# The w_down sums of a Strassen-like feed-forward: half of them beside attention, the rest in smaller steps, and a layer norm on three engines

## The chip, the cores and the metric

The kernel runs on one core of a Trainium2 chip. Its engines have instruction streams of their own: TensorE (PE in the profile, its weight loads PEld), VectorE (DVE), ScalarE (ACT), GpSimd (POOL) and SyncE (SP), which here issues all DMA transfers, in its own order. The metric is the device time in microseconds (us); lower is better. The comparison is by the median of several runs.

## The reference, cut to what matters

One layer of a decoder with 2048 tokens of width 1024, all in float32: four mixers, of which three feed `ymix` and the dilated attention feeds the rest of the columns, then an output projection, a layer norm, a feed-forward of width 4096 with a squared ReLU, and a second layer norm.

```python
mix = jnp.concatenate([y_a, y_b, y_c, y_d], axis=-1).astype(x.dtype) @ w_out[l]
x = _layer_norm(ALPHA * x + mix, ln1_w[l], ln1_b[l])
h = jnp.square(jax.nn.relu(x @ w_up[l]))
x = _layer_norm(ALPHA * x + h @ w_down[l], ln2_w[l], ln2_b[l])
```

## The kernel before, in words

Every matrix product runs as three products of rounded parts: an operand is split by ACT into a high part (names ending in `h`) and by VectorE or POOL into the rest (ending in `l`); the helper `split` (L169) gives every third rest to POOL. Elementwise helpers record all their operations in one line each: L115 for additions, subtractions and products of two tiles, L128 for the form with a scalar (`stt`), L131 and L135 for ACT, L112 for matrix products.

The order of the instructions is set by a scheduler that reads the program as it is written and places each instruction by its own estimate of when operands and buffers are free; what is written earlier has the higher priority. So a step written late may stand early on a queue, and the other way round. Engines then run their streams in that order. DMA is issued by SP alone.

The stages after the mixers:

- Attention (up to about 1690 us in the profile). `weave` puts steps of other work between its units: `out_part(t)` multiplies the first three mixers' columns of token tile t by `w_out` (six of the eight row blocks), and `out_final(t)` adds attention's columns, forms the first layer norm and stores the tile and its transpose (`x1`, `x1T`). A unit loads its values as `av`.
- The up projection, `ffn_up`, twice, for one half of the tokens each (1767 to 2493 us). It is a two-by-two scheme with seven products P1 to P7 in place of eight; the sums of operands are formed by VectorE and POOL. Each half has 16 steps `s`, one for 128 columns and their partner. A step loads four pieces of `w_up` (`wr`), forms sums, splits seven weights, runs seven products of 12 matrix instructions each, and stores seven results to DRAM (`H7`, in the trace `H0P..` and `H1P..`). A step starts its chain with a copy of P1 out of PSUM to `q`. The functions `mid(s)` and `between(s)` are called inside and behind a step, and run a step of another generator there.
- `ffn_x1`: sums and splits of the second half's inputs, behind the steps 8 to 11 of the first half.
- `ffn_t`: for each of 16 rows f it loads four pieces of `w_down` (`b12`, `t1`, `b22`, `b21`), forms four differences, and stores them as P5, P7, P6 and P4 in `TD` (the trace says `TDP`). It has two steps a row (load, then form and store). Three of its four buffers are `xr`, of which there are three; the fourth is `x1t`.
- The down projection, `ffn_down` (2493 us to the end): 32 steps of seven products each, 16 for each half of the tokens. Inputs are read back from `H7` and split (`hh`, `hl`), the weights of a product (`x0h`, `x1h` and so on) are exchanged every fourth step, each product at an offset of its own (`OFF`). The sums of products are added to `y`, which starts as ALPHA times the residual `x1`: ACT scales it on arrival, POOL adds `t`, `u2` or `u3` (the tiles `wh`), VectorE adds a product out of PSUM. Four groups of tokens go through four steps each in a half; in the last of them `lnorm2` runs on two tiles of 128 tokens, and the result is stored. Its `y` is then loaded with the residual of the other half.

Of the kernel before, what the change touches and what calls it, by code (L numbers as in the profile page):

```python
# [18 lines left out]
P = 128  # L19
# [65 lines left out]
class Body:  # L85
# [1006 lines left out]
    def out_open(self, es, ef):  # L1092
# [3 lines left out]
        self.zF = [self.dp.tile([P, D], F32, name=f"zF{t}") for t in range(seq // P)]  # L1096
        self.xT = [self.dp.tile([KT, P, 512], F32, name=f"x1T{i}") for i in range(seq // 512)]
# [76 lines left out]
    def ffn_open(self, es):  # L1174
# [8 lines left out]
        self.TD = {n: [self.dp.tile([P, 512], F32, name=f"TD{n}_{f}") for f in range(16)] for n in ("P4", "P5", "P6", "P7")}  # L1183
# [163 lines left out]
    def ffn_t(self):  # L1347

        nc, w = self.nc, self.ap["w_down"]
        for f in (12, 13, 14, 15, *range(12)):  # L1350
            b12, t1, b22 = self.raw(w[f][:, 512:]), self.raw(w[f][:, :512]), self.raw(w[f + 16][:, 512:])
            b21 = self.t(self.of, "x1t", [P, 2, 512], bufs=1)[:, 0]
            nc.sync.dma_start(b21, w[f + 16][:, :512])
            yield
            self.sub("v", t1, b12, t1)
            nc.sync.dma_start(self.TD["P5"][f], t1)
            self.sub("g", b12, b22, b12)
            nc.sync.dma_start(self.TD["P7"][f], b12)
            self.sub("v", b22, b22, t1)
            nc.sync.dma_start(self.TD["P6"][f], b22)  # L1360
            self.sub("g", b21, b21, b22)
# [6 lines left out]
    OFF = {"P1": 1, "P6": 1, "P2": 2, "P4": 2, "P5": 3, "P3": 3, "P7": 0}  # L1368

    def ffn_down(self):  # L1370

        nc, tc, of = self.nc, self.tc, self.of
        nsteps = 32
        wtag = lambda n: "x1" if n in ("P1", "P6", "P4", "P3") else "x0"
        chunk = lambda n, i: (i - self.OFF[n]) // 4 % 4
        with ExitStack() as es:
# [66 lines left out]
            for n, place in zip(("P1", "P6", "P2", "P5", "P7", "P4", "P3"), places):  # L1443
                if place == "xr":
                    W[n] = [self.split_to(wtag(n), r) for r in load_w(n, chunk(n, 0), place)]
                else:
                    split_w(n, list(load_w(n, chunk(n, 0), place)))
                if n == "P2":
                    for m in range(7):
                        load_h(m)  # L1450
                    lns = self.t(of, "ln1", [P, 2, D], bufs=1)
                    nc.sync.dma_start(lns, self.ap["lns"][2:4].partition_broadcast(P))
                    split_h(0)
                    split_h(1)
                elif n == "P7":
                    split_h(2)
                    split_h(3)
# [5 lines left out]
            for i in range(nsteps):  # L1463
# [50 lines left out]
def body(ctx, tc, ap, seq=SEQ):  # L1514
# [34 lines left out]
    def run(it):  # L1549
        for _ in it:  # L1550
            pass
# [138 lines left out]
```

## Time and profile before

| | |
|---|---|
| time, three runs | 3149.95 us median (3141.89 to 3160.94) |
| the profiled execution | 3160.75 us; its span, first to last instruction, 3159.0 us |
| PE | 2910.0 us busy, 92% of the span |
| VectorE, ACT, POOL | 69%, 43% and 50% |
| mean granted clock of TensorE | 0.927 |
| DMA | 513.71 MB, 163 GB/s in the mean |

Times within a stage are counted from the start of the span. Lines of the profile name an engine, a line of the source, the tile written and the tiles read, the count and a duration; a time in brackets is how long the engine stood idle before, and behind the arrow what ended it. Tables by stretch give the busy time of each engine, the granted clock as a share of full speed, and the mean busy share of the 16 DMA engines.

### The profile page before, as it was taken

The page shows a single profiled execution, that of the slowest core. Times are in us where ns is not written, and L with a number is a line of the kernel's source. Part 1 is how long each engine was busy: PE and PEld are TensorE (multiplying, and loading weights), DVE is VectorE, ACT ScalarE, POOL GpSimd, SP SyncE. Part 2 cuts the span into 40 slices and gives each one's busy share as a digit, 9 for nine tenths or more (in the row PEclk, how much of TensorE's full clock was granted, in tenths as well). Part 3 has the DMA queues.
Part 4 walks back from the last instruction along what each step waited for, and adds up shares of the span by engine and source line. Part 5 has one row for each costly group of instructions (what it writes and reads, how often), then busy time and mean ns, then how long its engine had stood idle before and what let it go on. Part 6 is the DMA issues. An engine that isn't in the chain of part 4 may idle for free. (4 is left out here: it accounts for less than half of the span.)

```text
span 3159.0 us, 46740 instructions
## 1 busy us (share of the span) xinstructions
PE 2910.0 (92%) x15524; PEld 2362.1 (75%) x15524; DVE 2193.9 (69%) x3828; ACT 1353.0 (43%) x2910; POOL 1571.1 (50%) x1432
## 2 busy tenths in 40 slices
PE   8889989889899999899998699898999899999997
PEld 6567777777778778777777578676778688877885
DVE  3457589776977865533445767778777677798878
ACT  3335333433443353334334354444354554454444
POOL 1333366454735645300123745556655476667765
PEclk9899798987999999699998799999999899999998
DMA  5344323333333354443455556777875766676653
GB/s 174 125 119 109 104 88 100 116 99 79 112 106 106 108 157 136 149 132 123 148 174 166 183 175 201 246 225 236 283 220 158 264 225 190 191 230 217 213 189 128
DMA packets 406657, 513.71 MB, mean 163 GB/s; under 512 B 34320, under 2 KB 234128, under 8 KB 406160
## 3 DMA queue, kind: packets, MB, share of 16 engines
q1 hardware_dynamic: 406416, 510.72, 52.0%
q8 instruction: 123, 2.02, 0.3%
q14 instruction: 118, 0.97, 0.1%
HBM read 354.69 MB, written 155.91 MB: 162 GB/s over the span
## 5 line engine op out<-in xcount | busy, mean ns | idle before, releaser
L112 PE MATMUL mm<-xh,wh 128*128 128x512 f32 x672 | 282.8, 423 | 33.3 <-ACT xh L135 17.8
L112 PE MATMUL mm<-xl,wh 128*128 128x512 f32 x672 | 282.1, 420 | 5.6 <-DVE xl L115 3.0
L112 PE MATMUL mm<-xh,wl 128*128 128x512 f32 x672 | 278.7, 415 | 2.7 <-DVE wl L115 2.6
L112 PE MATMUL bank<-x1h,hh 128*128 128x512 f32 x512 | 201.4, 393 | 16.9 <-ACT hh L135 12.3
L135 ACT ACTIVATE wh<-raw 128x512 fp32r<-128x512 f32 (+1 forms) x220 | 136.5, 629 | 172.2 <-DMA raw<-in_w_ch 68.8
L115 POOL TENSOR_TENSOR y<-y,wh 128x512 f32<-128x512 f32 x112 | 175.0, 1573 | 63.5 <-DVE wh L115 36.3
L112 PE MATMUL bank<-x1h,hl 128*128 128x512 f32 x512 | 200.9, 392 | 4.5 <-DVE hl L115 2.7
L112 PE MATMUL bank<-x1l,hh 128*128 128x512 f32 x512 | 200.9, 392 | 0.0
L112 PE MATMUL bank<-x0h,wh 128*128 128x512 f32 x384 | 159.2, 415 | 39.1 <-DVE c L115 30.5
L112 PEld LDWEIGHTS mm<-xh,wh 128*128 128x128 f32 x672 | 133.1, 198 | 73.5 <-ACT xh L135 22.8
L115 DVE TENSOR_TENSOR wl<-raw,wh 128x512 fp32r<-128x512 f32 (+1 forms) x146 | 124.4, 857 | 71.0 <-ACT wh L135 68.5
L115 POOL TENSOR_TENSOR wl<-raw,wh 128x512 fp32r<-128x512 f32 (+1 forms) x74 | 104.6, 1415 | 131.0 <-ACT wh L135 118.4
L112 PE MATMUL mm<-wh,xh 128*128 128x256 f32 (+1 forms) x512 | 156.9, 309 | 7.4 <-ACT stg L131 4.1
L112 PEld LDWEIGHTS mm<-xl,wh 128*128 128x128 f32 x672 | 132.9, 198 | 39.6 <-DVE xl L115 6.0
L112 PE MATMUL mm<-wl,xh 128*128 128x256 f32 (+1 forms) x512 | 156.7, 307 | 4.3 <-DVE wl L115 3.4
L112 PEld LDWEIGHTS mm<-xh,wl 128*128 128x128 f32 x672 | 132.7, 197 | 34.5 <-DVE wl L115 3.9
L112 PE MATMUL bank<-x0l,wh 128*128 128x512 f32 x384 | 156.4, 408 | 0.0
L112 PE MATMUL bank<-x0h,wl 128*128 128x512 f32 x384 | 155.8, 406 | 0.0
L112 PE MATMUL mm<-wh,xl 128*128 128x256 f32 (+1 forms) x512 | 154.4, 303 | 0.0
L112 PE MATMUL bank<-x0h,hh 128*128 128x512 f32 x384 | 150.4, 392 | 2.2 <-DVE y L128 1.3
L112 PE MATMUL bank<-x1h,wh 128*128 128x512 f32 x384 | 150.3, 392 | 2.1 <-ACT q L135 2.1
L112 PE MATMUL bank<-x0h,hl 128*128 128x512 f32 x384 | 150.3, 392 | 1.8 <-DVE hl L115 1.8
(466 smaller groups left out, 8801.9 us busy)
## 6 DMA issues: line engine op xcount, KB each, us to landing
raw<-in_w_ch SPq DMA_DIRECT2D x140, 256.0 KB, 3.0
wr<-in_w_up SPq DMA_DIRECT2D x128, 256.0 KB, 3.3
wl<-TDP SPq DMA_DIRECT2D x128, 256.0 KB, 3.5
wl<-in_w_down SPq DMA_DIRECT2D x104, 256.0 KB, 3.5
chF<-stg SPq DMA_DIRECT2D x68, 256.0 KB, 2.4
xraw<-in_xT SPq DMA_DIRECT2D x64, 256.0 KB, 3.7
z<-H0P SPq DMA_DIRECT2D x64, 256.0 KB, 4.1
z<-H1P SPq DMA_DIRECT2D x64, 256.0 KB, 3.8
```

What stands on the lines that cost most here:

```text
L112: return self.nc.tensor.matmul(out, lhsT, rhs, start=start, stop=stop)
L115: (self.nc.gpsimd if eng == "g" else self.nc.vector).tensor_tensor(out, a, b, op=op)
L135: self.nc.scalar.activation(out, in_, AF.Copy)
```

## The change

- `ffn_t` takes a list of rows and a mode. Rows 12 to 15 and 0 to 3 are formed in attention's first `weave`, by four steps in each of eight `out_part`s, in the two `z2` tiles, with all four subtractions on POOL. Rows 4 to 11 stay in the up projection with VectorE and POOL as before. A row now has four steps in place of two: load two pieces; subtract, store P5 and load the other two; subtract twice and store P7 and P6; subtract and store P4.
- In the up projection 12 of the remaining 32 steps are called in the first half and 20 in the second half's steps 2 to 11, two a step. Before these were 12 and 20 of 32 steps that were twice as long.
- At the start of `ffn_down` the inputs are loaded behind the second weight, and one input is split behind each of the second to fifth weights. P7 is prepared before P5; their `OFF` values are exchanged.
- The layer norm's weights (`lns`) are loaded in step 2, as written.
- The residual is no longer scaled by ACT. In the first step of a group the accumulation itself multiplies by ALPHA, and POOL's add follows it; in later steps the add comes first.
- `lnorm2` centres with ACT, scales with VectorE (`stt`, by the deviation and the weight), and adds the bias on VectorE for the first half of the columns and on POOL for the second.

```diff
-    def ffn_t(self):
+    def ffn_t(self, fs, up):
         nc, w = self.nc, self.ap["w_down"]
-        for f in (12, 13, 14, 15, *range(12)):
-            b12, t1, b22 = self.raw(w[f][:, 512:]), self.raw(w[f][:, :512]), self.raw(w[f + 16][:, 512:])
-            b21 = self.t(self.of, "x1t", [P, 2, 512], bufs=1)[:, 0]
+        e = "v" if up else "g"
+        for f in fs:
+            if up:
+                b12, t1, b22 = (self.t(self.fr, "xr", [P, 512], bufs=3) for _ in range(3))
+                b21 = self.t(self.of, "x1t", [P, 2, 512], bufs=1)[:, 0]
+            else:
+                (b12, t1), (b22, b21) = ((z[:, 0], z[:, 1]) for z in (self.t(self.of, "z2", [P, 2, 512], bufs=2) for _ in range(2)))
+            nc.sync.dma_start(b12, w[f][:, 512:])
+            nc.sync.dma_start(t1, w[f][:, :512])
+            yield
+            self.sub(e, t1, b12, t1)
+            nc.sync.dma_start(self.TD["P5"][f], t1)
+            nc.sync.dma_start(b22, w[f + 16][:, 512:])
             nc.sync.dma_start(b21, w[f + 16][:, :512])
             yield
-            self.sub("v", t1, b12, t1)
-            nc.sync.dma_start(self.TD["P5"][f], t1)
             self.sub("g", b12, b22, b12)
             nc.sync.dma_start(self.TD["P7"][f], b12)
-            self.sub("v", b22, b22, t1)
+            self.sub(e, b22, b22, t1)
             nc.sync.dma_start(self.TD["P6"][f], b22)
+            yield
             self.sub("g", b21, b21, b22)
             nc.sync.dma_start(self.TD["P4"][f], b21)
             yield
...
-    OFF = {"P1": 1, "P6": 1, "P2": 2, "P4": 2, "P5": 3, "P3": 3, "P7": 0}
+    OFF = {"P1": 1, "P6": 1, "P2": 2, "P4": 2, "P7": 3, "P3": 3, "P5": 0}
...
-            for n, place in zip(("P1", "P6", "P2", "P5", "P7", "P4", "P3"), places):
+            for q, (n, place) in enumerate(zip(("P1", "P6", "P2", "P7", "P5", "P4", "P3"), places)):
+                rs = load_w(n, chunk(n, 0), place)
...
-                if n == "P2":
+                if q == 1:
                     for m in range(7):
                         load_h(m)
-                    lns = self.t(of, "ln1", [P, 2, D], bufs=1)
-                    nc.sync.dma_start(lns, self.ap["lns"][2:4].partition_broadcast(P))
-                    split_h(0)
-                    split_h(1)
-                elif n == "P7":
-                    split_h(2)
-                    split_h(3)
+                if 0 < q < 5:
+                    split_h(q - 1)
...
-                            self.act(y[l][j], y[l][j], AF.Copy, scale=ALPHA)
-
-                def acc(l, j, ps, last=True):
-                    self.stt(y[l][j], y[l][j], 1.0, ps, ALU.mult, ALU.add, stat[:, tl[l], j : j + 1] if last and v == 3 else None)
+
+                def acc(l, j, ps, u=None, last=True):
+                    if u is not None and v:
+                        self.add("g", y[l][j], y[l][j], u)
+                    ps = ps()
+                    self.stt(y[l][j], y[l][j], 1.0 if v else ALPHA, ps, ALU.mult, ALU.add,
+                             stat[:, tl[l], j : j + 1] if last and v == 3 else None)
+                    if u is not None and not v:
+                        self.add("g", y[l][j], y[l][j], u)
...
+                if i == 2:
+                    nc.sync.dma_start(lns, self.ap["lns"][2:4].partition_broadcast(P))
...
-            self.stt(y, y, stat[:, 0:1], lns[:, 0, cs], ALU.add, ALU.mult)
-            self.stt(y, y, stat[:, 1:2], lns[:, 1, cs], ALU.mult, ALU.add)
+            self.act(y, y, AF.Identity, bias=stat[:, 0:1])
+            self.stt(y, y, stat[:, 1:2], lns[:, 0, cs], ALU.mult, ALU.mult)
+            self.add("vg"[j], y, y, lns[:, 1, cs])
...
+    T = B.ffn_t((12, 13, 14, 15, 0, 1, 2, 3), False)
+    def part_t(t):
+        for i, _ in enumerate(B.out_part(t)):
+            if i in (0, 2, 4, 6):
+                next(T)
+            yield
...
-        T = B.ffn_t()
-        B.ffn_up(0, X, lambda s: run(B.out_final(11 + s)) if 0 < s < 5 else next(X1) if 7 < s < 12 else None if s == 15 else next(T) if s > 4 else None,
-                 lambda s: next(T) if s in (6, 7, 8) or s > 12 else None)
-        loads = (2, 3, 4, 5, 7, 8, 9, 11, 12, 13)
-        B.ffn_up(1, next(X1), lambda s: next(T) if s in loads else None, lambda s: next(T) if s - 1 in loads else None)
+        T = B.ffn_t(range(4, 12), True)
+        B.ffn_up(0, X, lambda s: run(B.out_final(11 + s)) if 0 < s < 5 else next(X1) if 7 < s < 12 else next(T) if 4 < s < 8 else None,
+                 lambda s: [next(T) for _ in range(1 + (s == 8))] if 4 < s < 9 or s > 11 else None)
+        B.ffn_up(1, next(X1), lambda s: next(T) if 1 < s < 12 else None, lambda s: next(T) if 1 < s < 12 else None)
```

The order at three places. First SP's queue where attention begins, just behind the load of the first layer norm's weights; `od` are stores of attention's results. Before:

```order
L1109 DMA ln_2116_12527<-in_lns 128x2048
L474 DMA av_12122<-vF 128x256
L509 DMA od_12047<-ao_12052 128x264
L474 DMA av_12158<-vF 128x256
L509 DMA od_12047<-ao_12088 128x264
```

and now:

```order
L1110 DMA ln_2116_12591<-in_lns 128x2048
L1358 DMA z_2173_12722<-in_w_down 128x512
L1359 DMA z_2173_12722<-in_w_down 128x512
L1363 DMA z_2174_12723<-in_w_down 128x512
L1364 DMA z_2174_12723<-in_w_down 128x512
L1362 DMA TDP_12_12548<-z_2173_12722 128x512
L474 DMA av_12122<-vF 128x256
L509 DMA od_12047<-ao_12052 128x264
L1367 DMA TDP_12_12580<-z_2173_12722 128x512
L1369 DMA TDP_12_12564<-z_2174_12723 128x512
```

The first row of sums (f = 12) stands here, its loads and first store ahead of the next values `av`. Eight rows lie between this place and the last `out_part` of the first `weave`.

Second, SP's queue in the up projection, second half, where the first result of its second group of four steps (`H1P_1`) is stored. Before:

```order
L1315 DMA H1P_1_15402<-q_3537_20141 512x1x128
L1353 DMA x1t_21449<-in_w_down 128x512
L1356 DMA TDP_9_15454<-xr_21445 128x512
L1358 DMA TDP_9_15486<-xr_21443 128x512
L1360 DMA TDP_9_15470<-xr_21447 128x512
L1270 DMA wr_20447<-in_w_up 128x512
L1196 DMA xr_21616<-in_w_down 128x512
L1362 DMA TDP_9_15438<-x1t_21449 128x512
L1270 DMA wr_20449<-in_w_up 128x512
L1196 DMA xr_21618<-in_w_down 128x512
L1315 DMA H1P_1_15414<-c_20144 512x1x128
```

and now:

```order
L1315 DMA H1P_1_15578<-q_3537_20197 512x1x128
L1270 DMA wr_20487<-in_w_up 128x512
L1315 DMA H1P_1_15590<-c_20200 512x1x128
L1270 DMA wr_20489<-in_w_up 128x512
L1315 DMA H1P_1_15582<-u_3539_20199 512x1x128
L1270 DMA wr_20491<-in_w_up 128x512
```

The sums are done by then. Counted between the loads of `wr`, the queue has 42 loads of `w_down` over six steps of the second half before, at seven or eight in most steps, and now 22 over three, at the same density; in the first half 12 stores of sums behind the second half's inputs have become four.

Third, POOL at the start of the down projection; `u` are the last step's results of the up projection, `x1l` the rests of the weights of P3, `hl` those of the inputs. Before:

```order
L115 TENSOR_TENSOR u_3834_22005<-q_3833_22004,u_3834_22005 128x512
L115 TENSOR_TENSOR u_3835_22006<-u_3835_22006,q_3833_22004 128x512
L115 TENSOR_TENSOR x1l_22320<-wl_22309,x1h_22319 128x512
L115 TENSOR_TENSOR hl_22280<-z_3882_22211,hh_22279 128x512
L115 TENSOR_TENSOR hl_22359<-z_3882_22211,hh_22358 128x512
```

and now:

```order
L115 TENSOR_TENSOR u_3818_21989<-q_3817_21988,u_3818_21989 128x512
L115 TENSOR_TENSOR x1l_22303<-wl_22292,x1h_22302 128x512
L115 TENSOR_TENSOR u_3819_21990<-u_3819_21990,q_3817_21988 128x512
L115 TENSOR_TENSOR hl_22179<-xr_22166,hh_22178 128x512
L115 TENSOR_TENSOR hl_22263<-z_3855_22172,hh_22262 128x512
```

The `hl` of the very first product (from an `xr` tile) was on VectorE, behind the rests of the weights of P3, and is now on POOL. On ACT all the `hh` stand behind the last split of a weight, before and now.

More of the change, by code (lines that the diff above doesn't have):

```diff
@@ L1096, in out_open @@
         self.zF = [self.dp.tile([P, D], F32, name=f"zF{t}") for t in range(seq // P)]
+        self.TD = {n: [self.dp.tile([P, 512], F32, name=f"TD{n}_{f}") for f in range(16)] for n in ("P4", "P5", "P6", "P7")}
         self.xT = [self.dp.tile([KT, P, 512], F32, name=f"x1T{i}") for i in range(seq // 512)]
@@ L1182, in ffn_open @@
         self.H7 = [{n: [self.dp.tile([P, 4, 4, P], F32, name=f"H{hf}{n}_{c}") for c in range(4)] for n in PN} for hf in range(2)]
-        self.TD = {n: [self.dp.tile([P, 512], F32, name=f"TD{n}_{f}") for f in range(16)] for n in ("P4", "P5", "P6", "P7")}
     def new(self, tag):
@@ L1373, in ffn_down @@
         nsteps = 32
+        lns = self.t(of, "ln1", [P, 2, D], bufs=1)
         wtag = lambda n: "x1" if n in ("P1", "P6", "P4", "P3") else "x0"
@@ L1442, in ffn_down @@
             places = ("xr", "xr", "wl", "wh", "wl", "wh", "wl")
-            for n, place in zip(("P1", "P6", "P2", "P5", "P7", "P4", "P3"), places):
+            for q, (n, place) in enumerate(zip(("P1", "P6", "P2", "P7", "P5", "P4", "P3"), places)):
+                rs = load_w(n, chunk(n, 0), place)
                 if place == "xr":
-                    W[n] = [self.split_to(wtag(n), r) for r in load_w(n, chunk(n, 0), place)]
+                    W[n] = [self.split_to(wtag(n), r) for r in rs]
                 else:
-                    split_w(n, list(load_w(n, chunk(n, 0), place)))
-                if n == "P2":
+                    split_w(n, list(rs))
+                if q == 1:
                     for m in range(7):
                         load_h(m)
-                    lns = self.t(of, "ln1", [P, 2, D], bufs=1)
-                    nc.sync.dma_start(lns, self.ap["lns"][2:4].partition_broadcast(P))
-                    split_h(0)
-                    split_h(1)
-                elif n == "P7":
-                    split_h(2)
-                    split_h(3)
+                if 0 < q < 5:
+                    split_h(q - 1)
             for m in (7, 8, 9):
@@ L1479, in ffn_down @@
                 self.add("v", u2, t, prod(m + 1))
-                self.add("g", y[0][0], y[0][0], t)
-                acc(0, 0, prod(m + 2))
-                self.add("g", y[0][1], y[0][1], u2)
+                acc(0, 0, lambda: prod(m + 2), t)
                 self.add("v", u3, u2, prod(m + 3))
                 p5 = prod(m + 4)
-                self.add("g", y[1][1], y[1][1], u3)
-                acc(0, 1, p5, False)
-                acc(1, 1, p5)
-                self.add("g", y[1][0], y[1][0], u3)
-                acc(1, 0, prod(m + 5))
-                acc(0, 1, prod(m + 6))
+                acc(0, 1, lambda: p5, u2, False)
+                acc(1, 1, lambda: p5, u3)
+                acc(1, 0, lambda: prod(m + 5), u3)
+                self.stt(y[0][1], y[0][1], 1.0, prod(m + 6), ALU.mult, ALU.add, stat[:, tl[0], 1:2] if v == 3 else None)
+                if i == 2:
+                    nc.sync.dma_start(lns, self.ap["lns"][2:4].partition_broadcast(P))
                 if v == 3:
@@ L1589, in body @@
     part = lambda t: (B.out_part(t), 7)
+    T = B.ffn_t((12, 13, 14, 15, 0, 1, 2, 3), False)
[4 more added lines that the diff above has]
+            yield
     final = lambda t: (B.out_final(t, "tp"), 1)
-    B.weave(marks, units[12:24], [part(t) for t in range(8)])
+    B.weave(marks, units[12:24], [(part_t(t), 7) for t in range(8)])
     for q in (0, 4):
```

## The prediction

> **What bounds the kernel now.** I read the page's busy shares first, then a table of busy time by stretch, then the copies that mark the steps of the up projection, then who waits for whom.
>
> ```profile
> PE 2910.0 (92%) x15524; PEld 2362.1 (75%) x15524; DVE 2193.9 (69%) x3828; ACT 1353.0 (43%) x2910; POOL 1571.1 (50%) x1432
> ```
>
> TensorE is busy for 92% of the span, so a gain must come out of the 249 us in which it is idle, or out of stretches at a lower clock. The stretches below tell where these lie. The columns are the stretch, its length, busy time of PE, PEld, DVE, ACT and POOL, the granted clock, the DMA share and GB/s.
>
> ```profile
> 1332.00:1500.00 168.00, 167.11 (x838) 133.31 (x838) 59.36 (x278) 65.23 (x254) 3.85 (x14) 0.96 0.42 132
> 1942.00:2084.00 142.00, 125.90 (x525) 102.24 (x524) 106.31 (x115) 59.63 (x105) 87.43 (x59) 0.95 0.83 260
> 2166.00:2331.00 165.00, 149.02 (x607) 118.85 (x606) 131.18 (x140) 70.77 (x128) 101.17 (x69) 0.94 0.86 272
> 2331.00:2478.00 147.00, 146.25 (x639) 119.42 (x638) 105.45 (x127) 73.35 (x131) 72.35 (x51) 1.00 0.53 159
> 2478.00:2511.00 33.00, 17.98 (x74) 14.00 (x73) 23.76 (x26) 19.19 (x35) 17.57 (x13) 0.80 0.99 332
> 2760.00:2860.00 100.00, 89.85 (x375) 71.60 (x375) 93.77 (x135) 53.77 (x108) 63.85 (x44) 0.97 0.70 226
> 2860.00:3080.00 220.00, 220.00 (x972) 182.18 (x971) 174.81 (x201) 105.80 (x180) 157.18 (x102) 1.00 0.64 204
> 3131.00:3159.00 28.00, 6.56 (x28) 4.79 (x26) 20.71 (x40) 7.30 (x18) 10.56 (x10) 0.71 0.20 75
> ```
>
> Attention with its fills (1332 to 1500) is full on TensorE, with POOL almost empty. The up projection loses time in two stretches, 1942 to 2084 (the second half's inputs and some of the w_down sums) and 2166 to 2331 (ten of the sixteen w_down rows); between 2331 and 2478, without sums, it loses nothing. The down projection loses time at its start (2478 to 2511), where its halves meet (2760 to 2860) and in the tail. One copy of a PSUM bank to `q` stands in each step of the up projection, so first, last and count give the length of a step:
>
> ```profile
> L135 ACT ACTIVATE q<-bank x7: 576/578/591, 1942.3 to 2084.3; 128x512 f32<-128x512 f32 x7
> L135 ACT ACTIVATE q<-bank x8: 572/575/578, 2166.3 to 2331.4; 128x512 f32<-128x512 f32 x8
> L135 ACT ACTIVATE q<-bank x9: 574/579/581, 2331.4 to 2477.5; 128x512 f32<-128x512 f32 x9
> ```
>
> That is 142.0/6 = 23.7 us, 165.1/7 = 23.6 us and 146.1/8 = 18.3 us a step. A step beside the sums costs 5.3 us more than one without. The waits of 2140 to 2331 and the traffic of 2166 to 2331 say why:
>
> ```profile
> PE bank L112 <- DVE c L115: 13.7, 6, 4.4
> DVE u L115 <- DMA H1P<-u: 4.3, 3, 2.6
> ...
> xr<-in_w_down SPq DMA_DIRECT2D x34, 256.0 KB, 4.3
> TDP<-xr SPq DMA_DIRECT2D x30, 256.0 KB, 3.4
> ```
>
> TensorE waits for a bank that VectorE has not read yet, and VectorE is late behind stores of its own results and the sums: the DMA share is 0.86 against 0.53, and a load lands in 4.3 us.
>
> **The change, part by part.** The sum is made against the profiled execution, 3160.75 us (span 3159.0 and 1.75 around it). The median of the three runs, 3149.95, is 10.8 lower; I take the same difference off the median.
>
> *Eight rows of sums go beside attention.* Each row is four subtractions, four loads and four stores of 256 KB. All four are on POOL there; the same operations in the up projection give their price:
>
> ```profile
> L115 DVE TENSOR_TENSOR xr<-xr,xr x20: 678/692/1783, 2177.7 to 2303.8; 128x512 f32<-128x512 f32 x20
> L115 POOL TENSOR_TENSOR xr<-xr,xr x10: 1268/1298/1745, 2180.7 to 2302.1; 128x512 f32<-128x512 f32 x10
> L115 POOL TENSOR_TENSOR x1t<-x1t,xr x10: 1262/1298/1742, 2183.2 to 2304.6; 128x512 f32<-128x512 f32 x10
> ```
>
> 32 x 1.30 = 42 us of POOL, which has 168.0 - 3.9 = 164 us free in the stretch. 64 transfers are 16.8 MB; over 168 us 100 GB/s on top of 132, less than the 272 of the sums' stretch. The first rows begin before 1332 by the order, which only spreads them. What could suffer are VectorE's steps of attention and the SP queue:
>
> ```profile
> L487 DVE CUSTOM_DVE_ANT_0 aS<-bank,abias x86: 280/286/425, 1331.7 to 1492.8; 128x128 f32<-128x128 f32 x62, 128x256 f32<-128x256 f32 x24
> ...
> SPq L474 <- PE bank L112: 35.7, 12, 7.7
> ...
> av<-vF SPq DMA_DIRECT2D x15, 128.0 KB, 2.2
> ```
>
> The queue's own waits there are for TensorE to free the buffer of the next values `av`, so it has time to give; 21 units (x86 reductions, four a unit) in 168 us are 8 us each, and an `av` load lands in 2.2. Each row of sums holds the queue for at most a landing (4.3) and four subtractions (5.2), 9.5 us, but `av` loads stand between its stores. I take 0, with -1 and +10 as ends (a tenth of the 76 us that eight rows could hold it, and rounding). The Trainium skill ("GPSIMD Engine Reference", section "Engine selection") would keep elementwise work of two inputs on VectorE, as about twice slower on GpSimd. The rows agree on the ratio (1.30 against 0.69), but the engine is idle; by that rule alone the move would cost 32 x 0.6 = 20 us of engine time, none of it on TensorE's path.
>
> *Second half of the up projection.* Ten rows become five. The order shows the rows bunched as before, about two a step, over some three steps in place of six. Three steps at 5.3 less make -16; the last one still has the first weights of the down projection to split (they follow the sums closer), so I take -14. Ends: -37 (all seven steps lose their 5.3) and 0.
>
> *First half.* Six rows become three: one stays ahead of the steps, one falls beside the inputs, one behind. In the stretch 1942 to 2084 the excess is 6 x 5.4 = 32 us, with five rows (40 transfers) beside 28 transfers of the inputs. Now two rows stay. By transfers 24/68 of it would go, -11; but the inputs' own sums are done in the same order and stay. I take -5, ends -11 and 0.
>
> *Start of the down projection.* The code puts a split of inputs behind each of four weights. On ACT the order did not follow: `hh` still stands behind all twenty splits of weights, and 332 GB/s at a share of 0.99 says that the transfers bind here; their bytes are the same. What moved is the first `hl`, from VectorE to POOL:
>
> ```profile
> 2505.95 0.79 PE L112 MATMUL bank<-x1h,hh 128*128 128x512 f32 x1 [12.34 <-ACT hh L135]
> 2510.70 0.79 PE L112 MATMUL bank<-x1h,hl 128*128 128x512 f32 x1 [2.68 <-DVE hl L115]
> ...
> 2504.91 4.06 DVE L115 TENSOR_TENSOR x1l<-wl,x1h 128x512 fp32r<-128x512 f32 x3
> 2508.89 3.43 DVE L115 TENSOR_TENSOR hl<-xr,hh 128x512 fp32r<-128x512 f32 x2
> ...
> 2505.07 1.66 POOL L115 TENSOR_TENSOR u<-u,q 128x512 f32<-128x512 f32 x1 [1.23 <-DVE q L115]
> ```
>
> `hl` follows POOL's `u` directly: it starts at 2506.7 in place of 2508.9. I take -2, ends -8 (half of 12.3 and the 2.7) and +3 (if POOL's `u` is late by as much). The offsets of P5 and P7 are exchanged, so P7 starts with the last quarter of the rows and P5 with the first; that changes no count and no byte: 0.
>
> *Where the halves meet.* The residual is no longer scaled by ACT (32 copies), but by the first accumulation; the layer norm's four VectorE operations a tile become two, with two more on ACT and one add each on VectorE and POOL.
>
> ```profile
> ACT y L131 <- DMA y<-x: 35.8, 11, 7.2
> ...
> L131 ACT ACTIVATE y<-y x28: 614/632/637, 2515.1 to 2853.2; 128x512 f32<-128x512 f32 x28
> L128 DVE SCALAR_TENSOR_TENSOR y<-y,st,ln x56: 735/750/1791, 2761.9 to 3152.3; 128x512 f32<-128x512 f32 x56
> L115 POOL TENSOR_TENSOR y<-y,wh x112: 1283/1678/1863, 2520.1 to 3137.7; 128x512 f32<-128x512 f32 x112
> ```
>
> From 2760 to 2860 ACT stood 35.8 us before residuals that had not landed, with the splits for TensorE behind them. That wait goes; VectorE takes it at the accumulation, later by one product. VectorE is the full engine here (93.8 of 100): eight tiles give it 8 x 0.75 = 6 us less, and POOL 8 x 1.68 = 13 more. TensorE idles 10.2. I take -4, ends -10 (all of it) and +9 (each add holds a VectorE operation up for the 1.0 between 750 and 1791, and one more us).
>
> *Tail.*
>
> ```profile
> 3147.94 0.72 ACT L131 ACTIVATE ya<-y,st 128x512 bf16<-128x512 f32 x1 [11.88 <-DVE st L1498]
> ...
> 3150.65 0.99 POOL L115 TENSOR_TENSOR st<-st,mhalf 128x1 f32<-128x1 f32 x1 [4.63 <-DVE st L1504]
> 3153.90 0.55 POOL L115 TENSOR_TENSOR st<-st,mhalf 128x1 f32<-128x1 f32 x1 [2.26 <-DVE st L1504]
> ...
> 3154.48 1.41 DVE L128 SCALAR_TENSOR_TENSOR x1t<-x1t,st,ln 128x512 f32<-128x512 f32 x2 [0.66 <-POOL st L115]
> ```
>
> Now two centrings by ACT (0.63 each) stand ahead of the second tile's squares, an add stands on POOL between its two powers, and an add of 1.3 behind the last scaling: about +3. VectorE reaches this point with two operations of 0.75 to 1.79 less behind it: -2. I take +1, ends -2 and +4.
>
> Sum: 0 - 14 - 5 - 2 - 4 + 1 = -24, so 3136.75 for the profiled execution and 3126 for the median.
>
> **Rivals.**
>
> All of it hidden: the code gives a row of sums two steps where it had one, and half as many rows may fit beside the products as the plain steps do. For it: 2331 to 2478 has a DMA share of 0.53. Against it: the order bunches them as before. The up projection then gives 7 x 5.3 = 37 and 7, and with -5 for the rest the time is 3101.
>
> The sums were not the cause: the steps are long because of the inputs' reloads and the stores of the products, and stay so. For it: the stretch 1942 to 2084 has steps as long with fewer rows. Then only -2 - 4 + 1 is left: 3145, no change that can be told.
>
> The port: the adds moved to POOL hold VectorE up. For it: the same scaling takes 735 to 750 ns or up to 1791, and POOL's add 1283 or up to 1863. With +9 where the halves meet in place of -4, and +4 in the tail for +1, the time is 3142. The Trainium skill ("SBUF — State Buffer", section "Who interferes with whom") says that a VectorE instruction with two SBUF inputs and a GpSimd one that reads SBUF block each other; the trace agrees with its 750 against 1791. By that rule the layer norm gains little from POOL, though attention's reductions out of PSUM are safe.
>
> The other side, SP's queue in attention: stores of sums wait for POOL, and `av`, `ym` and the residual queue behind them. It decides where a hold outlasts the slack of an `av` load. Eight rows hold the queue for up to 9.5 each, 76 us. If a whole unit of 8 us is the slack, 1.5 a row or 12 us are lost; if there is next to none, some 65 us reach TensorE, and the time is 3126 + 65 = 3191. Against it stands that the queue itself waits 35.7 us for TensorE there.
>
> **How the numbers follow.** Half a per cent, 16 us, is what a measurement can tell, so faster means below 3134 and slower above 3166. Chances: the forecast 0.42, all hidden 0.16, not the cause 0.20, the port 0.11, the queue 0.11. Below 3134 fall 0.35 of the first, all 0.16, 0.03 of the third and 0.02 of the fourth: 0.56. Above 3166 fall 0.09 of the queue and 0.02 of the middle ones: 0.11. The rest is 0.33. The range reaches from the case of all hidden to the one in which nothing is, 3099 to 3150, and leaves out the queue and the forecast's far ends.
>
> **What would show it.** In the changed kernel, steps by the copies to `q` should be long in about three steps of the second half and 18.3 in the others; the DMA share beside attention should rise to about 0.7 with TensorE still full; `hl` should start at most 2 us behind `hh` at the down projection's start; ACT's wait for `y` should be gone where the halves meet; the tail from TensorE's last product should stay near 20 us. I am wrong if steps without sums stay long, if attention's stretch grows by more than 10 us, or if the meeting of the halves gets longer.

## The result, and the profile after

The changed kernel took 3140.31 us in the median of 17 runs, and the kernel before 3160.94 us in the median of 17 runs beside them: a ratio of 0.9942 over all these runs, with a 95% interval of 0.9921 to 0.9962. By this ratio it is 18 us less (12 to 25; the two medians lie 20.6 apart); 24 less had been forecast. The profiled execution has a span of 3137.7 us, against 3159.0.

The busy shares of the changed kernel, first block of its page:

```profile
PE 2891.4 (92%) x15524; PEld 2350.8 (75%) x15524; DVE 2162.9 (69%) x3796; ACT 1353.5 (43%) x2910; POOL 1610.1 (51%) x1464
```

TensorE is idle for 246 us, against 249: the shares hardly tell that anything happened. The table by stretch of the changed kernel does, with the columns as in the prediction: attention, the second half's inputs, the steps with sums, the steps without, the start of the down projection, the meeting of the halves, the steps behind it, the tail.

```profile
1316.00:1484.00 168.00, 166.77 (x848) 134.09 (x848) 63.65 (x274) 63.42 (x251) 31.39 (x42) 0.96 0.63 200
1918.00:2076.00 158.00, 142.45 (x600) 116.11 (x599) 108.41 (x130) 68.75 (x122) 86.49 (x59) 0.95 0.70 216
2142.00:2267.00 125.00, 108.47 (x446) 87.08 (x445) 99.64 (x113) 60.59 (x110) 73.29 (x50) 0.95 0.83 259
2267.00:2457.00 190.00, 190.00 (x832) 155.86 (x831) 130.91 (x158) 94.35 (x164) 91.53 (x65) 1.00 0.52 153
2457.00:2493.00 36.00, 23.15 (x89) 18.12 (x88) 24.82 (x28) 21.86 (x39) 19.32 (x14) 0.81 0.95 318
2738.00:2838.00 100.00, 91.00 (x386) 72.84 (x385) 90.15 (x126) 59.51 (x117) 71.94 (x50) 0.97 0.69 223
2838.00:3058.00 220.00, 220.00 (x971) 181.97 (x971) 175.28 (x204) 103.44 (x177) 160.78 (x107) 1.00 0.64 207
3109.50:3137.70 28.20, 6.12 (x27) 4.72 (x26) 15.81 (x34) 11.76 (x26) 13.67 (x12) 0.69 0.19 74
```

TensorE is still full beside attention, with a DMA share of 0.63 in place of 0.42. The stretch with sums is 125 us in place of 165, and the full stretch behind it 190 in place of 147. (The two are not cut at the same step: from the 17th copy to `q`, where the stretch of before begins, the one with sums is 108.) Nothing moved visibly where the halves meet.

Not all of the 21 us between the two spans is the change's. Both kernels issue the same instructions in the same order on every engine up to attention (the first that differs is SP's first load of sums, at 1277 us in the changed kernel), and yet TensorE's 8001st product started at 1344.1 us before and at 1327.9 after. A second trace of the kernel before was taken for this:

> The kernel before once more, for a second trace. If the 16 us by which the traces of before and after differ at 1330 us are chance (their instructions are in the same order until then), this trace stands at another place there than the first, by up to 16 us either way; if they belong to the kernel, within 3 us of the first trace (first product of attention's step at 1344.1 us).

It stands there at 1339.2, and fourteen traces of all kernels of this study lie between 1325.1 and 1345.4 (the latest is of a kernel with sums beside attention, the earliest of one without). Three rows by stretch tell why; they are of the kernel before, its second trace, and the changed kernel:

```profile
355.00:400.00 45.00, 45.00 (x243) 36.22 (x242) 18.02 (x40) 12.35 (x26) 10.58 (x11) 0.62 0.29 68
```

```profile
355.00:400.00 45.00, 45.00 (x232) 35.76 (x232) 17.61 (x37) 11.20 (x31) 10.18 (x10) 0.58 0.31 70
```

```profile
355.00:400.00 45.00, 45.00 (x300) 37.43 (x298) 25.83 (x50) 14.95 (x32) 18.13 (x18) 0.84 0.29 68
```

In the same 45 us TensorE is busy throughout, but finishes 243, 232 or 300 products, since the granted clock was 0.62, 0.58 or 0.84. By the growth of the distance between two traces across it, such a spell of half clock costs 7 to 11 us, and it comes at other places in other runs. So single spans can't be subtracted here. Below, stages are compared from the 8001st product on, by the places of the same products and of the copies to `q`. The second trace of the changed kernel is that of the run with later calls (below), whose engines issue the same instructions in the same order:

| stage (us) | before, two traces | changed, two traces | difference | forecast |
|---|---|---|---|---|
| attention and handover: 8001st product to 5th copy to `q` | 550.3, 550.8 | 557.9, 554.2 | +5.5 | 0 |
| first half of the up projection: to the 16th copy | 245.3, 247.1 | 245.6, 238.6 | -4.1 | -5 |
| second half: to the 32nd copy | 337.8, 339.5 | 325.5, 325.3 | -13.2 | -14 |
| start of the down projection: to its 201st product | 79.7, 79.5 | 77.7, 78.2 | -1.6 | -2 |
| halves meet: its 1101st to 1751st product | 162.7, 163.2 | 160.4, 160.4 | -2.6 | -4 |
| last group and tail: to the end | 235.1, 235.1 | 238.7, 238.6 | +3.6 | +1 |
| sum | | | -12.4 | -24 |

The stretch that the table leaves out, from the 201st to the 1101st product of the down projection, is 204.0 us in all four traces. The sum of the stages, -12.4, lies at the edge of the timed -12 to -25; with two traces a side, and the first half alone differing by 7 us between two traces of one program, more isn't to be had from them.

### The profile page after: what moved, and what is told of

It reads as the page before. It is cut to its first block, busy times and chain, and to the rows that moved or that the text cites. A ratio compares the mean times of both kernels' runs of the same rounds, so it can differ in the third digit from the quotient of the medians.

```text
span 3137.7 us, 46732 instructions
## 1 busy us (share of the span) xinstructions
PE 2891.4 (92%) x15524; PEld 2350.8 (75%) x15524; DVE 2162.9 (69%) x3796; ACT 1353.5 (43%) x2910; POOL 1610.1 (51%) x1464
## 4 chain that ended last, share of the span: by engine, by line
PE 56%; DVE 17%; DMA 12%; issue 6%; POOL 5%; ACT 4%; SPq 1%; POOLq 0%; DVEq 0%; ACTq 0%
PE bank L112 37%; PE mm L112 16%; DMA xraw<-in_xT 2%; PE bank L157 2%; DVE wl L115 2%; DVE hgQ L115 1%; DVE rzp L115 1%; DMA raw<-in_w_ch 1%; DVE stg L128 1%; DVE rZc L115 1%; DMA wr<-in_w_up 1%; DMA H0P<-u 1%; DVE x1l L115 1%; DVE u L115 1%; ACT wh L135 1%
## 5 line engine op out<-in xcount | busy, mean ns | idle before, releaser
L112 PE MATMUL bank<-x1h,hh 128*128 128x512 f32 x512 | 200.3, 391 | 10.8 <-ACT hh L135 10.8
L112 PE MATMUL bank<-x1l,wh 128*128 128x512 f32 x384 | 151.3, 394 | 4.6 <-POOL x1l L115 2.7
```

The lines of the kernel that those rows point to most:

```text
L112: return self.nc.tensor.matmul(out, lhsT, rhs, start=start, stop=stop)
```

## The experiments

**The two parts of the change, each alone.** The first has the changed sums with `ffn_down` and `lnorm2` of before; the second has the sums of before.

```diff
  (t_only)     changed kernel, but OFF, ffn_down and lnorm2 as before
  (down_only)  kernel before, but OFF, ffn_down and lnorm2 as changed
```

> The changed sums and their places, with the down projection and the layer norm as before. Theory A (a row of sums costs 3.6 us on TensorE's path in the up projection, so five rows fewer in its second half give -12; the traces' difference ahead of 1330 us is chance): from the first to the last copy to q of the second half 325 us in place of 338; attention with the handover to the up projection 0 to +7; in all -5 to -18, a ratio of 0.994 to 0.998. Theory B (the gain lies in the down projection, the steps are long for another reason): second half 335 or more, ratio 1.000.

> The changed start of the down projection, accumulation and layer norm, with all sums where they were. Theory A: start of the down projection -2, meeting of the halves -2, tail +3; second half of the up projection 338 as before; in all -1, a ratio of 0.998 to 1.001. Theory B: most of the gain is here, ratio 0.995 or less.

Measured: the sums alone 0.9938 (0.9915 to 0.9962), the down projection alone 0.9986 (0.9966 to 1.0007). The second half took 323.1 us and 336.3. So the gain is the sums' and theory B falls; the changes in the down projection together are worth nothing that can be timed.

**All sixteen rows beside attention.**

```diff
-    T = B.ffn_t((12, 13, 14, 15, 0, 1, 2, 3), False)
+    T = B.ffn_t((12, 13, 14, 15, *range(12)), False)
...
-            if i in (0, 2, 4, 6):
-                next(T)
+            for _ in range(1 + (i == 3)):
+                next(T)
```

The calls for sums in the up projection are gone.

> The changed kernel with all sixteen rows of sums beside attention and none in the up projection. Theory A: the four long steps of the second half (93 us) become 18.6 each, so 307 us from the first to the last copy to q in place of 325; attention takes 64 more transfers and 42 us more of POOL with +0 to +10; ratio to the kernel before 0.986 to 0.993. Theory B (the long steps come from the reloads of inputs and the stores of products): 325 stays, ratio 0.994. A third way (SP's queue and the transfers saturate in attention): second half 307, but attention longer by 20 us or more.

Measured: 0.9941 (0.9915 to 0.9966), no better than eight rows, so the ratio of theory A was missed; the trace is nearest to the third way, a longer attention. The second half took 316.7 us in place of 325.5, the first 233.1 in place of 242, but attention with the handover 570.2 in place of 556. To see what a row costs, the trace is cut at every 84th product of TensorE, since 84 make a step. The first ten steps of the second half (us):

| | |
|---|---|
| before, ten rows | 27.1, 23.2, 24.0, 19.2, 25.9, 23.1, 20.2, 24.9, 20.1, 19.6 |
| changed, five rows | 27.8, 21.2, 26.1, 19.2, 24.8, 19.2, 19.2, 19.2, 19.2, 19.2 |
| no rows (this run) | 27.5, 25.3, 19.2, 19.2, 19.2, 19.2, 19.2, 19.2, 19.2, 19.2 |

A plain step is 19.2. Above that, ten rows lose 35 us, five rows 23, and none still 14 (in the other traces of such steps 34 and 37 with ten rows, 19 to 23 with five): the first two steps are long with no sums. That the second half's inputs, which are formed just ahead, make them long was not tested. A row costs 1 to 2 us, and theory A was right in kind; its 307 forgot these two steps.

**Where the sums stand in the second half.** First, the calls for them written four steps later:

```diff
-        B.ffn_up(1, next(X1), lambda s: next(T) if 1 < s < 12 else None, lambda s: next(T) if 1 < s < 12 else None)
+        B.ffn_up(1, next(X1), lambda s: next(T) if s > 5 else None, lambda s: next(T) if s > 5 else None)
```

> The changed kernel with the calls for the sums of the second half written in steps 6 to 15 in place of 2 to 11. The scheduler puts every instruction where it was (the order of SP and of TensorE is the same row by row), so this is a second trace of the changed kernel: from TensorE's 8001st product on 1803 to 1810 us (the first trace 1809.8), the place of that product by chance within 1325 and 1345. If the writing of small steps mattered by itself, the second half would be other than 323 to 326 us.

The second half took 325.3 us, and from the 8001st product on the trace is 1799.3, a little less than the 1803 expected at the least. Every engine issues the same instructions in the same order as without this edit, so the place in the program isn't what puts the sums there: the scheduler issues a step as soon as its buffers are free, and the small steps are bunched like the large ones. To hold them back, a column of the running step's `q` was copied into the tiles ahead of their loads:

```diff
+            def late(*ts):
+                if up and self.pace is not None:
+                    for t in ts:
+                        self.copy("v", t[:, :1], self.pace[:, :1])
+
+            late(b12, t1)
...
+            late(b22, b21)
```

This was done with five rows in the second half, with eight rows in the second and none in the first, and with all sixteen in the up projection and none beside attention.

> The changed kernel, but each load of a row of sums in the second half of the up projection first waits for that step's P1 (a copy of one column of it into the tile to be loaded), so the five rows lie one half row a step behind the fourth step instead of bunched in the first five. Measured from one step's first product on TensorE to the next, 15 steps of the second half are 19.2 us at the least; over that the changed kernel loses 23 us, and 14 us without any sums. Theory C (a row costs TensorE only where it meets the reloads of inputs at the half's start; beside plain steps it is hidden): 14 us, all losses in the first three steps; 9 us less than the changed kernel, ratio to before 0.991. Theory A (a row costs 1.7 us wherever it stands): 23 us as before, spread over ten steps, ratio 0.994.

> The changed kernel with no sums in the first half of the up projection and eight rows in the second, held to its steps in the same way. The first half takes 313 us from its second step on as without sums, in place of 327. Theory C: the second half loses 14 to 16 us over 19.2 a step; 21 us less than the changed kernel in all, ratio to before 0.987. Theory A: the second half loses 14 + 8 x 1.7 = 28; 7 us less than the changed kernel, ratio 0.992.

> The changed kernel with no sums beside attention: all sixteen rows in the up projection, held to its steps in both halves, two and a quarter of a row in three steps where they stand. Attention with the handover goes back by 7 us. Theory C: losses of the second half 14 to 18, of the first half as without sums (313): 28 us less than the changed kernel, ratio to before 0.985. Theory A: losses of 14 + 11 x 1.7 = 33 and 320: about as the changed kernel, ratio 0.994. A third way: two thirds of a row a step is past what VectorE and the transfers can take, steps of 21 us and ratio 1.00 or more.

Measured: 1.0015 (0.9992 to 1.0038), 1.0034 (1.0007 to 1.0060) and 1.0133 (1.0093 to 1.0173). Both theories failed, C by the sign; of the third run, the third way (a ratio of 1.00 or more) came true. With five rows the steps from the fifth on are 22.1, 19.3, 22.7, 21.2, 19.2, 23.7, 20.5, 19.2, 25.2, 27.1: 28 us for rows that cost 9 when bunched. The waits of this kernel over the second half, and then those of the changed kernel (who waited for whom, us, times, longest):

```profile
ACT c L131 <- DVE c L115: 70.5, 14, 7.6
...
PE bank L112 <- DVE c L115: 23.1, 9, 5.2
...
DVE xr L115 <- POOL xr L115: 15.3, 5, 3.8
DVE xr L115 <- DMA xr<-in_w_down: 13.9, 5, 3.0
```

```profile
ACT c L131 <- DVE c L115: 33.7, 10, 8.0
...
PE bank L112 <- DVE c L115: 15.2, 4, 5.3
...
DVE xr L115 <- POOL xr L115: 2.3, 1, 2.3
DVE xr L115 <- DMA xr<-in_w_down: 1.3, 1, 1.3
```

VectorE itself now stands before POOL's subtraction (15.3 us in five waits) and before the row's own loads (13.9 in five), 29 us in place of 4, and what is behind it in its queue, `c`, keeps a bank from TensorE nine times in place of four. Bunched, a row's operands are there when its subtraction comes up; held back, they are not yet. The small copies that hold the rows back stand in VectorE's queue too, and their own share was not told apart. Whether rows that are spread without such waits would be hidden was not tried.

**The layer norm.** The changed kernel with the `lnorm2` of before, and with both adds on VectorE:

```diff
-            self.act(y, y, AF.Identity, bias=stat[:, 0:1])
-            self.stt(y, y, stat[:, 1:2], lns[:, 0, cs], ALU.mult, ALU.mult)
-            self.add("vg"[j], y, y, lns[:, 1, cs])
+            self.stt(y, y, stat[:, 0:1], lns[:, 0, cs], ALU.add, ALU.mult)
+            self.stt(y, y, stat[:, 1:2], lns[:, 1, cs], ALU.mult, ALU.add)
```

```diff
-            self.add("vg"[j], y, y, lns[:, 1, cs])
+            self.add("v", y, y, lns[:, 1, cs])
```

> The changed kernel with the layer norm of before (two VectorE operations a half of the columns, no ACT, no adds). Theory P (the adds on POOL hold VectorE's two-input operations up in the last group, so TensorE waits 2.9 us for hl): that wait falls to 0.3, last product 3 us earlier, the tail 0.7 shorter, in all -3 to -4. If the layer norm also brought the 2.8 us gained where the halves meet, that comes back and the total is 0; if the accumulation brought it, it stays. Rival: the wait stays at 2.9, since the accumulation's new order makes hl late.

> The changed kernel with both adds of the layer norm's bias on VectorE, none on POOL. Theory P (POOL's adds hold VectorE's two-input operations up): the last 938 products of TensorE take 213.2 us as with the old layer norm in place of 216.3, where the halves meet 158.6 in place of 160.4; 4 to 5 us less than the changed kernel. Rival (it is the longer chain, with one hop more between ACT and VectorE, and more operations on VectorE): 216 or more stay, and the tail grows by 1.

Measured: 0.9929 (0.9905 to 0.9954) and 0.9960 (0.9935 to 0.9986); beside the changed kernel's 0.9942 neither is told apart by time. The traces do it (us):

| | halves meet | last group | tail |
|---|---|---|---|
| before | 162.7 | 213.3 | 21.8 |
| changed | 160.4 | 216.3 | 22.5 |
| changed, old layer norm | 158.6 | 213.2 | 20.4 |
| changed, adds on VectorE | 161.7 | 217.3 | 21.2 |

By these traces the new accumulation gains 4.1 + 0.1 + 1.4 = 5.6, and the new layer norm gives back 1.8 + 3.1 + 2.1 = 7.0. The last version below has the old layer norm with the new accumulation too, with 161.3, 213.2 and 20.7: it repeats the 5 us that the new layer norm costs in the last group and the tail, but not the 1.8 where the halves meet, nor the full 4.1 there. TensorE's wait in the last group, in the changed kernel and in the one with adds on VectorE:

```profile
PE bank L112 <- DVE hl L115: 2.9, 1, 2.9
```

```profile
PE bank L112 <- DVE hl L115: 2.8, 1, 2.8
```

With the old layer norm no wait for `hl` is left there. Theory P was right on the place but not on the cause: with no add on POOL the wait stays. What VectorE does ahead of that `hl`, in the changed kernel, then with the old layer norm, then with both adds on VectorE:

```profile
3092.63 3.49 DVE L128 SCALAR_TENSOR_TENSOR y<-y,st,ln 128x512 f32<-128x512 f32 x2 [1.70 <-POOL st L115]
3096.05 0.68 DVE L115 TENSOR_TENSOR wh<-wh,bank 128x512 f32<-128x512 f32 x1
3096.64 1.40 DVE L115 TENSOR_TENSOR x0l<-wl,x0h 128x512 fp32r<-128x512 f32 x1
3097.97 1.77 DVE L115 TENSOR_TENSOR y<-y,ln 128x512 f32<-128x512 f32 x1
3099.66 1.75 DVE L115 TENSOR_TENSOR hl<-xr,hh 128x512 fp32r<-128x512 f32 x1
```

```profile
3102.00 3.48 DVE L128 SCALAR_TENSOR_TENSOR y<-y,st,ln 128x512 f32<-128x512 f32 x2 [0.44 <-POOL st L115]
3105.41 1.78 DVE L115 TENSOR_TENSOR hl<-xr,hh 128x512 fp32r<-128x512 f32 x1
```

```profile
3088.20 1.78 DVE L115 TENSOR_TENSOR y<-y,ln 128x512 f32<-128x512 f32 x1
...
3090.51 1.78 DVE L115 TENSOR_TENSOR y<-y,ln 128x512 f32<-128x512 f32 x1
...
3095.83 3.46 DVE L128 SCALAR_TENSOR_TENSOR y<-y,st,ln 128x512 f32<-128x512 f32 x2
3099.21 1.75 DVE L115 TENSOR_TENSOR hl<-xr,hh 128x512 fp32r<-128x512 f32 x1
```

The old form centres and weighs ahead of the deviation and has one operation a half behind it, two in all (3.48). The new one keeps scaling and adding for behind the deviation: the same two (3.49), then the add (1.77). Counted from the 1751st product of the down projection, where the last group begins, this `hl` starts at 200.7 us in the changed kernel, at 197.6 with the old layer norm and at 200.6 with both adds on VectorE. In the changed kernel the scalings start where they do with the old form (193.7 and 194.2), but the add and two other operations, together 3.6 us, come between them and `hl`. With both adds on VectorE nothing comes between, but the scalings start only at 197.2, two adds (1.78 each) having stood ahead of them. So it is what VectorE's queue holds ahead of `hl` that makes it late, whichever engine has the second add. In either form these operations take some 1.75 us each there, with POOL at work on operands in SBUF, where the shortest of their kind take 0.68 to 0.75; that it is POOL which stretches them is read from this coincidence, as in the prediction's rows.

**The engine of the sums beside attention.**

```diff
-        e = "v" if up else "g"
+        e = "v"
...
-            self.sub("g", b12, b22, b12)
+            self.sub("g" if up else "v", b12, b22, b12)
...
-            self.sub("g", b21, b21, b22)
+            self.sub("g" if up else "v", b21, b21, b22)
```

> The changed kernel with the four subtractions of each row beside attention on VectorE in place of POOL. If the engine is what costs there, attention with the handover (from TensorE's 8001st product to the fifth copy to q, 554 us in the mean of five traces with sums there, 551 without) changes: theory G (POOL is idle there and VectorE has attention's reductions) 558 or more, ratio 0.995; theory V (a two-input operation belongs on VectorE, 0.69 in place of 1.30 us) 551 or less, ratio 0.992; if transfers and the order of the fills cost, it stays at 553 to 557.

Measured: 0.9953 (0.9931 to 0.9974), not told apart from the changed kernel. In its one trace attention with the handover took 545.2 us, as theory V had it. TensorE's order differs here from the 7863rd product on; counted from the 7801st, ahead of any difference, it is 598.0, against 603.0 to 609.2 in six traces with POOL's subtractions and 600.3 and 600.7 in those of before. The Trainium skill ("GPSIMD Engine Reference", section "Engine selection") prefers VectorE for such operations. This trace goes its way for the stage, and the time of the whole does not show it. The loss itself lies at the end of the stage. The stretches from 360 us behind the 8001st product to the fifth copy to `q`, of the kernel before, the changed one, the one with sixteen rows, this one, and the one with eight rows held back in the second half:

```profile
1704.00:1894.00 190.00, 155.68 (x662) 123.68 (x661) 130.25 (x231) 89.65 (x196) 103.13 (x123) 0.82 0.57 178
```

```profile
1688.00:1886.00 198.00, 157.04 (x619) 121.18 (x619) 128.19 (x217) 81.65 (x173) 101.74 (x115) 0.80 0.53 166
```

```profile
1691.00:1901.00 210.00, 167.60 (x667) 125.01 (x666) 133.81 (x234) 88.81 (x181) 111.58 (x138) 0.81 0.52 164
```

```profile
1704.00:1889.00 185.00, 155.19 (x665) 122.49 (x663) 126.74 (x233) 89.39 (x196) 104.02 (x123) 0.86 0.59 183
```

```profile
1705.00:1895.00 190.00, 151.99 (x606) 117.70 (x605) 126.44 (x210) 82.33 (x171) 98.78 (x115) 0.81 0.52 161
```

The rows beside attention are done long before; the last of their stores starts 62 us behind the 8001st product, with sixteen rows 164. What is formed here are the first sums of the up projection, which the scheduler puts into the handover: a row but for its last difference, and the first of the next. The kernel before has them (f = 12) as the changed one does (f = 4), and so has the one with VectorE. The traffic of the changed kernel's stretch:

```profile
xr<-in_w_down SPq DMA_DIRECT2D x5, 256.0 KB, 3.2
TDP<-xr SPq DMA_DIRECT2D x4, 256.0 KB, 2.0
```

This is where the changed kernel loses: 41 us of TensorE's idle time against 34 before. Attention's units ran ahead beside the sums (224 of its score products by 160 us behind the 8001st product, before 220; 228 with sixteen rows), and at the end the last token tiles' merges and norms stand alone. One wait stands out, for the first weights of the up projection; it is shown for the changed kernel from 1684 to 1784 us, for the kernel before from 1700 to 1840, and for the one with eight rows held back from 1705 to 1895:

```profile
PE bank L112 <- ACT wh L135: 9.2, 1, 9.2
```

```profile
PE bank L112 <- ACT wh L135: 2.7, 1, 2.7
```

```profile
PE bank L112 <- ACT wh L135: 9.4, 1, 9.4
```

The last of these runs tells what it is worth. Up to 1760 us of the changed kernel it issues the same instructions in the same order on every engine, the eight rows beside attention among them; there the changed kernel's queue has the first load of the sums in the handover, and it has none. It has the same long wait, and its stage took 549.4 us, against 553.1 to 557.9 in the six traces whose program is the changed kernel's up to here, and 550.3 to 551.4 in the three with the program of before. So, in this one trace, eight rows beside attention cost nothing by themselves, and the wait for `wh` is not the price either; the loss needs the sums in the handover behind them. Why the kernel before forms such sums there without it is open.

**A version from these results.** Twelve rows beside attention, none in the first half, four in the second, and the old layer norm with the new accumulation:

```diff
-    T = B.ffn_t((12, 13, 14, 15, 0, 1, 2, 3), False)
+    T = B.ffn_t((12, 13, 14, 15, *range(8)), False)
...
-            if i in (0, 2, 4, 6):
+            if i < 6:
```

The calls for sums in the up projection and `lnorm2` are changed as well.

> The old layer norm with the new accumulation, twelve rows of sums beside attention, none in the first half of the up projection and four in the second. Expected: attention with the handover 559 (554 with eight rows, 570 with sixteen), first half 233 as with sixteen, second half 323, down projection as with the old layer norm: 10 us less than the changed kernel in the middle of the traces, ratio to before 0.990. Rival (what attention gives back grows faster): attention 566 or more, ratio 0.993, no better than the old layer norm with eight rows.

Measured: 3115.65 us, 0.9874 (0.9834 to 0.9914), the fastest here. Attention with the handover took 546.6 us where 559 had been expected, the first half 230.8, the second 323.6, the last group and the tail 233.9. From the 8001st product on that is 1779.3 us, 37.7 less than the mean of the two traces before, and 40 less are timed (27 to 52). No sums stand in the handover here. That twelve rows then cost attention nothing, like the eight held back, and sixteen cost 20, says that the price does not follow the rows' transfers or POOL's time. That it is the order in which the scheduler lets the fills run out is a guess: no run changed that order alone.

## Why the prediction was right, point by point

- **Attention, 0 (-1 to +10): +5.5.** The cover named held: TensorE was full (166.8 of 168) and POOL idle enough. What was missed lies 200 us later, in the handover: with eight rows beside attention and the first sums of the up projection there the stage is longer, with the eight rows alone it was not (549.4).
- **Second half, -14: -13.2.** Right in size, from a reading that was off: the copies to `q` gave 5.3 a step by comparing steps that lag with steps that catch up (18.3 us, where TensorE needs 19.2), and charged the sums with 14 us that two steps lose with no sums at all. That rows are bunched was right (four of the first five steps are long, where three had been forecast); three steps at a wrong 5.3 came near the 12 us that five rows fewer save, so the size is in part luck.
- **First half, -5: -4.1**, with 7 us between two traces; without any rows it would have been -13 to -15.
- **Start, -2: -1.6.** TensorE still waits for `hh`, 10.8 us for 12.3, and for `hl` 2.1 for 2.7; POOL's `hl` follows `hh`, but its wait is for VectorE's. The reason given carries only these 0.6. The rest is not explained: with the sums alone and the old down projection the start took 77.8 us too, with 10.7 before `hh` and 2.65 before `hl`, and with the new down projection alone 78.2. In the changed kernel:

```profile
2484.09 0.79 PE L112 MATMUL bank<-x1h,hh 128*128 128x512 f32 x1 [10.78 <-ACT hh L135]
2489.08 0.80 PE L112 MATMUL bank<-x1h,hl 128*128 128x512 f32 x1 [2.06 <-DVE hl L115]
```

- **Halves meeting, -4: -2.6.** It is the down projection's: 160.4 us with its change alone, 163.2 with the sums alone. ACT's 35.8 us before `y` are gone, but ACT then stands before the weights' loads. In the kernel before (2760 to 2860) and then in the changed one (2738 to 2860):

```profile
ACT x1h L135 <- DMA wl<-TDP: 4.2, 3, 3.7
```

```profile
ACT x1h L135 <- DMA wl<-in_w_down: 18.8, 4, 8.7
ACT x1h L135 <- DMA wl<-TDP: 13.0, 5, 8.4
```

- **Tail, +1 (-2 to +4): +3.6 with the last group.** This term was mis-sized, and its reason turned round: the layer norm was taken to relieve VectorE, but its adds stand ahead of `hl` there, and it costs 5 us over the last group and the tail, of which the accumulation gives back little over 1. The rival of the port had the place and the size of it (+4 for the tail), though not its cause, so that was luck.
- **The profiled execution.** 3136.75 was forecast for its time and 3139.47 came, but 16 of the 21 us lie ahead of the change and are the clock's. The forecast that counts is the median's, -24 against a measured -18 (-25 to -12): right in direction and about a third too large, by the traces for the +5.5 at attention's end and the layer norm above all. Its 3126 is 14 us low as a time, most of it because the kernel before came out at 3160.94 in 17 runs, and not at the 3149.95 of the three.
- **Rivals.** All hidden: the second half would have lost 14, and lost 23. Not the cause: the sums alone are worth 0.9938. The queue: TensorE never ran dry beside the sums.

## What to carry to other kernels

Before two profiles are subtracted, look for the first instruction in which the programs differ, and count from there: here three quarters of the difference stood ahead of it. Measure a step by the engine that bounds it, not by a copy on another engine that may lag. Work moved beside a full stage is cheap while the stage lasts (TensorE stayed at 166.8 of 168 us); look at its end, and at what the scheduler puts into the handover behind it, and time a few splits, because the price there did not follow the amount: nothing with twelve rows and 20 us with sixteen, in one trace each.

## What the runs showed of the hardware

Spells of half clock of 24 to 41 us come at different places in programs that issue the same instructions: the kernel before had them near 361 us in both traces and near 736 in one, and the one with the changed down projection at 851. First the two traces of the kernel before, then the changed down projection:

```profile
730.00:780.00 50.00, 48.22 (x272) 37.00 (x271) 28.30 (x65) 15.04 (x35) 16.65 (x20) 0.70 0.31 75
```

```profile
730.00:780.00 50.00, 47.81 (x342) 37.91 (x342) 35.90 (x84) 19.23 (x45) 23.68 (x25) 0.93 0.34 85
```

```profile
845.00:900.00 55.00, 54.91 (x275) 42.27 (x274) 31.99 (x62) 18.07 (x37) 12.15 (x14) 0.63 0.31 75
```

In six other traces the last of these stretches has 0.91. Another spell, of 41 to 51 us, does not move: all fourteen traces have it between the 7801st and the 7990th product. In the kernel before, with TensorE busy for 45 of 47 us:

```profile
1293.00:1340.00 47.00, 45.23 (x185) 37.27 (x185) 20.82 (x96) 22.71 (x84) 3.74 (x3) 0.50 0.33 107
```

Runs of one kernel spread over 29 us (3126.9 to 3155.6 for the changed one). The Trainium skill ("TensorE: Matmul & The Clock Gate", section "What's actually happening") has the clock go back to full after one busy window of about 3.4 us. These rows differ: by the profile TensorE was busy for 45.00 of 45.00 us and had 0.58. The profiles do not show what sets the spells off.
